# Making the low halves of weight chunks with an accumulating DMA instead of a VectorE subtraction

## The chip, the cores and the metric

One NeuronCore of a Trainium2 chip runs the whole program. The time is device microseconds from start to end of one execution; the number that counts is the median over several executions.

## What is computed

A two-layer encoder trunk on one sequence of 512 tokens, width 1024, all in float32. Each layer is a half-step SwiGLU feed-forward block (22 tiles of 128 hidden units), a token mixer (windowed attention beside dilated attention, 8 heads each) and a second feed-forward block. Every block is pre-normed and shifted, scaled and gated by vectors that come from a conditioning vector `c` (the "ada" weights):

```python
for l in range(DEPTH):
    mod = (c_act @ ada_w[l] + ada_b[l]).reshape(b, N_MOD, 1, D_MODEL)
    h = modulate(rmsnorm(x, norm_ffn1[l]), sh1, sc1)
    x = x + 0.5 * g1 * swiglu(h, ffn1_wi[l], ffn1_wo[l])
    h = modulate(rmsnorm(x, norm_mix[l]), sh2, sc2)
    x = x + g2 * token_mixing(h, cos, sin, w_in[l], sink[l], onorm_a[l], onorm_b[l], w_out[l])
    h = modulate(rmsnorm(x, norm_ffn2[l]), sh3, sc3)
    x = x + 0.5 * g3 * swiglu(h, ffn2_wi[l], ffn2_wo[l])
return rmsnorm(x, final_norm)
```

## The kernel before, in words

TensorE multiplies in a reduced float32 format, so every operand is split into a high part (the value rounded to that format) and a low part (the value minus its high part), and each product is three matmuls: high by high, low by high, high by low (`mm3`, lines 213 to 217). TensorE needs both parts of a weight.

**Weights come in chunks.** `specs` (lines 98 to 126) lists all weight chunks in the order of their use: 128 partitions by up to 1024 numbers, that is up to 512 KB. A *plain* chunk is one array; a *pair* is two, turned into more matrices by a recursive scheme (`emit_pair`, lines 153 to 195), which the change leaves alone. `emit_chunk` (lines 128 to 148) loads a plain chunk into a `raw` tile (4 buffers) through SP's DMA queue (line 142), makes `hi` on ScalarE (line 146) and `lo` on VectorE (line 147); `hi` and `lo` have 6 buffers each, shared with the pairs. The indexes in `finer` (line 105: three before and six after the start of each block) are done in two halves of 512.

**Which chunks there are.** Chunks 0 to 5 are converted by `start` (lines 903 to 938). Of the other plain ones 45 are in `finer` and 161 are not: 89 of 1024 columns, 64 of 896, 4 of 960 and 4 of 640. The first feed-forward block of layer 0 has no pairs at all: its chunks 6 to 64 are 59 of the 161. Every other feed-forward block has 21 to 24 of them (all `wo`), each mixer 18.

**What sets the order.** A scheduler lays down each engine's instruction order at build time, from the program order, priorities and buffer counts; at run time each engine's and each DMA queue's instructions issue in that order. SP issues all DMAs of the kernel before: weight chunks, the ada columns (`ada_col`, line 297, 4 `araw` buffers in the first block and one in the later ones), and in the mixers the copies that spread rotated queries and keys (lines 587 to 598). An ada column is multiplied by `c` and summed on VectorE (line 302); 73 of these loads fall into the first feed-forward block after its opening. GpSimd (POOL) does two elementwise operations per rotated query or key in the mixers (lines 577 and 581) and little else. `ahead` (line 206) emits the next chunks in program order, three ahead of use.

TensorE's results wait in 4 PSUM buffers `mm`; in feed-forward blocks ScalarE (`sg`, `gh`, lines 499, 507, 525) and VectorE (`x`, `sg`, `gl`, lines 366, 496, 506, 510) empty them.

Of the kernel before, what the change touches and what calls it, by code (L numbers as in the profile page):

```python
# [10 lines left out]
F32 = mybir.dt.float32  # L11
F32R = mybir.dt.float32r
I32 = mybir.dt.int32
AF = mybir.ActivationFunctionType
ALU = mybir.AluOpType
# [44 lines left out]
def tile_trunk(ctx: ExitStack, tc: tile.TileContext, xT, c, positions, adaT, cols, sink, wi1, wo1,  # L60
               wqk, wv, w_out, wi2, wo2, masks, freqs, out):
    nc = tc.nc
    V, A, T, G = nc.vector, nc.scalar, nc.tensor, nc.gpsimd
# [35 lines left out]
    finer = set()  # L99
    live = {}  # L100
# [27 lines left out]
    def emit_chunk(pieces=1):  # L128
        i = state["emit"]
        if i >= len(specs):  # L130
            return
        if isinstance(specs[i], tuple):
            for _ in emit_pair():
                pass
            return
        state["emit"] += 1
        ap = specs[i]
        n = ap.shape[1]
        raw = wp.tile([128, 1024], F32, tag="raw", name="raw", bufs=4)
        hi = wp.tile([128, 1024], F32R, tag="hi", name="hi")  # L140
        lo = wp.tile([128, 1024], F32R, tag="lo", name="lo")
        nc.sync.dma_start(raw[:, :n], ap)
        step = 512 if i in finer else n
        for a in range(0, n, step):
            sl = slice(a, min(a + step, n))
            A.activation(hi[:, sl], raw[:, sl], AF.Copy)  # L146
            V.tensor_tensor(lo[:, sl], raw[:, sl], hi.bitcast(F32)[:, sl], op=ALU.subtract)  # L147
        live[i] = (hi, lo)

    def parts(t):  # L150
        return [t[:, a:a + 512] for a in (0, 512)]
# [1 line left out]
    def emit_pair():  # L153


        i = state["emit"]
        state["emit"] += 1
        pool = temps[0]
        rg, ru = (wp.tile([128, 1024], F32, tag="raw", name="raw", bufs=4) for _ in range(2))
        for r, ap in zip((rg, ru), specs[i]):  # L160
            nc.sync.dma_start(r, ap)
        hs = [wp.tile([128, 1024], F32R, tag="hi", name="hi") for _ in range(3)]
        ls = [wp.tile([128, 1024], F32R, tag="lo", name="lo") for _ in range(3)]
        ta = pool.tile([128, 1024], F32, tag="ta", name="ta")
        h4 = pool.tile([128, 512], F32R, tag="h4", name="h4")
        l4 = pool.tile([128, 512], F32R, tag="l4", name="l4")
        live[i] = (*zip(hs, ls), (h4, l4))
        b11, b21 = parts(rg)
        b12, b22 = parts(ru)
        t1, t2 = parts(ta)  # L170

        def high(dst, src):
            for d, r in zip(parts(dst), parts(src)):
                A.activation(d, r, AF.Copy)  # L174

        def low(dst, src, h):
            V.tensor_tensor(dst, src, h.bitcast(F32), op=ALU.subtract)

        high(hs[0], rg)
        V.tensor_tensor(t1, b12, b11, op=ALU.subtract)  # L180
        yield
        V.tensor_tensor(t2, t1, b22, op=ALU.subtract)
        yield
        low(ls[0], rg, hs[0])
        yield
        high(hs[1], ta)
        V.tensor_tensor(b21, b21, t2, op=ALU.add)
        A.activation(h4, b21, AF.Copy)
        V.tensor_tensor(b12, b22, b12, op=ALU.subtract)
        low(ls[1], ta, hs[1])  # L190
        yield
        high(hs[2], ru)
        low(l4, b21, h4)
        yield
        low(ls[2], ru, hs[2])
# [3 lines left out]
    def chunk():  # L199
        i = state["use"]  # L200
        state["use"] += 1
        while state["emit"] <= min(i, len(specs) - 1):
            emit_chunk()
        return live.pop(i)

    def ahead(n=LA):
        while state["emit"] < len(specs):
            due = sum(3 if isinstance(specs[i], tuple) else 1 for i in range(state["use"], state["emit"]))
            if due > 1 if isinstance(specs[state["emit"]], tuple) else due >= n:
                return  # L210
            emit_chunk()
# [902 lines left out]
```

## Time and profile before

| what | value |
|---|---|
| median of 3 runs | 1957.17 us (1954.87 to 1959.26) |
| the profiled execution, its own time | 1955.42 us |
| its span, first to last instruction | 1953.6 us |
| mean granted TensorE clock | 0.993 of full speed |
| bytes moved by DMA | 267.98 MB, 41.8% of 16 engines' span on SP's queue |

The profiled execution is 1.8 us under the median, 0.09%. The span leaves 1.8 us of its own time outside the first and last instruction. Engine names in rows: PE is TensorE, PEld its weight loads, DVE VectorE, ACT ScalarE, POOL GpSimd, SPq the DMA queue that SyncE issues. A line number is that of the kernel. Matmul ends are modelled: a row's length holds the pipeline, while the distance of two starts tells the pace.

### The profile page before, as it was taken

How to read it: one execution, taken by the hardware profiler on the slowest of the kernel's cores; microseconds unless marked ns; L12 is line 12 of the kernel's file. 1: busy time of each engine (PE TensorE's matmuls, PEld its weight loads, DVE VectorE, ACT ScalarE, POOL GpSimd, SP SyncE). 2: the span in 40 equal slices, each digit the busy share in tenths (PEclk: the TensorE clock that was granted, in tenths of full speed). 3: DMA queues.
4: the chain of work that ended last, by engine and by line, in shares of the span. 5: the costliest groups of instructions: out<-in, count | busy, mean ns of one | idle time of the engine just before them, and what ended most of it. 6: DMA issues, size and time to landing. Idle time of an engine off the chain costs nothing.

```text
span 1953.6 us, 31187 instructions
## 1 busy us (share of the span) xinstructions
PE 1915.1 (98%) x12064; PEld 1718.1 (88%) x12064; DVE 1510.1 (77%) x2713; ACT 939.2 (48%) x1798; POOL 94.9 (5%) x69
## 2 busy tenths in 40 slices
PE   7999999999999999999999999999999999999998
PEld 5788888898778999989999897999977899898998
DVE  7988833477798988889589797876778989686773
ACT  5422222246585644536445262553556856353552
POOL 4000000011210000000000000000212000000000
PEclk8999999999999999999999999999999999999999
DMA  7889833244422154553415554242534113233231
GB/s 257 294 303 324 315 108 97 74 124 119 132 60 69 65 193 164 185 181 124 136 55 165 171 167 156 87 141 79 151 108 119 44 44 104 102 106 120 85 112 44
DMA packets 85111, 267.98 MB, mean 137 GB/s; under 512 B 10721, under 2 KB 13921, under 8 KB 84962
## 3 DMA queue, kind: packets, MB, share of 16 engines
q1 hardware_dynamic: 84962, 265.98, 41.8%
q8 instruction: 95, 1.56, 0.3%
q14 instruction: 54, 0.44, 0.1%
HBM read 244.97 MB, written 2.10 MB: 126 GB/s over the span
## 4 chain that ended last, share of the span: by engine, by line
PE 77%; DMA 9%; DVE 8%; issue 3%; ACT 2%; SPq 1%; POOL 0%; DVEq 0%; ACTq 0%; POOLq 0%
PE mm L217 14%; PE mm L216 14%; PE mm L215 14%; PE mm L457 9%; PE mm L458 8%; PE mm L459 8%; DMA araw<-in_adaT_dram 8%; DVE araw L302 3%; PE ptr L685 2%; DVE lo L147 1%; PE po L692 1%; PE po L693 1%; PE s L655 1%; PE s L656 1%; PE mm L624 1%
## 5 line engine op out<-in xcount | busy, mean ns | idle before, releaser
L146 ACT ACTIVATE hi<-raw 128x1024 fp32r<-128x1024 f32 (+5 forms) x251 | 213.8, 867 | 293.8 <-PE mm L217 201.8
L147 DVE TENSOR_TENSOR lo<-raw,hi 128x1024 fp32r<-128x1024 f32 (+5 forms) x251 | 258.1, 1039 | 74.3 <-ACT hi L146 73.4
L215 PE MATMUL mm<-hh,hi 128*128 128x512 f32 (+1 forms) x864 | 307.2, 357 | 7.4 <-ACT hh L286 6.8
L217 PE MATMUL mm<-hl,hi 128*128 128x512 f32 (+1 forms) x864 | 304.4, 357 | 2.7 <-DVE hl L287 2.7
L216 PE MATMUL mm<-hh,lo 128*128 128x512 f32 (+1 forms) x864 | 306.3, 356 | 0.0
L215 PE MATMUL mm<-gh,hi 128*128 128x512 f32 (+1 forms) x832 | 298.2, 358 | 5.5 <-ACT gh L507 5.5
L217 PE MATMUL mm<-gl,hi 128*128 128x512 f32 (+1 forms) x832 | 298.5, 359 | 0.5 <-DVE gl L441 0.2
L216 PE MATMUL mm<-gh,lo 128*128 128x512 f32 (+1 forms) x832 | 298.2, 358 | 0.0
L457 PE MATMUL mm<-sh,hi 128*128 128x256 f32 x912 | 260.4, 286 | 3.3 <-ACT sc L479 2.6
L458 PE MATMUL mm<-sh,lo 128*128 128x256 f32 x912 | 258.0, 283 | 0.0
L459 PE MATMUL mm<-sl,hi 128*128 128x256 f32 x912 | 257.9, 283 | 0.0
L302 DVE CUSTOM_DVE_ANT_0 araw<-araw,cs 128x1024 f32<-128x1024 f32 x136 | 167.7, 1236 | 57.9 <-DMA araw<-in_adaT_dram 57.5
L174 ACT ACTIVATE hi<-raw 128x512 fp32r<-128x512 f32 x228 | 132.9, 623 | 142.9 <-issue 74.3
L215 PEld LDWEIGHTS mm<-hh,hi 128*128 128x128 f32 x864 | 164.6, 191 | 29.9 <-ACT hh L286 8.1
L366 DVE SCALAR_TENSOR_TENSOR x<-mm,fin,x 128x512 f32<-128x512 f32 (+1 forms) x156 | 101.8, 653 | 114.3 <-PE mm L217 113.8
L217 PEld LDWEIGHTS mm<-hl,hi 128*128 128x128 f32 x864 | 164.1, 191 | 25.7 <-DVE hl L287 4.0
L215 PEld LDWEIGHTS mm<-gh,hi 128*128 128x128 f32 x832 | 157.8, 190 | 29.5 <-ACT gh L507 6.8
L216 PEld LDWEIGHTS mm<-hh,lo 128*128 128x128 f32 x864 | 164.5, 191 | 21.2
L217 PEld LDWEIGHTS mm<-gl,hi 128*128 128x128 f32 x832 | 158.1, 190 | 25.3 <-DVE gl L510 1.8
L457 PEld LDWEIGHTS mm<-sh,hi 128*128 128x128 f32 x912 | 174.1, 191 | 4.6 <-ACT sc L479 3.0
L216 PEld LDWEIGHTS mm<-gh,lo 128*128 128x128 f32 x832 | 158.1, 190 | 22.1
L458 PEld LDWEIGHTS mm<-sh,lo 128*128 128x128 f32 x912 | 174.3, 191 | 0.0
(188 smaller groups left out, 4043.7 us busy)
## 6 DMA issues: line engine op xcount, KB each, us to landing
raw<-in_wi_dram SPq DMA_DIRECT2D x170, 512.0 KB, 3.3
araw<-in_adaT_dram SPq DMA_DIRECT2D x144, 512.0 KB, 4.6
raw<-in_wo_dram SPq DMA_DIRECT2D x64, 448.0 KB, 4.1
raw<-in_wo_dram SPq DMA_DIRECT2D x32, 512.0 KB, 3.6
raw<-in_wqk_dram SPq DMA_DIRECT2D x26, 512.0 KB, 3.4
raw<-in_w_out_dram SPq DMA_DIRECT2D x16, 512.0 KB, 3.3
kh<-qh SPq DMA_DIRECT2D x40, 128.0 KB, 2.4
kl<-t SPq DMA_DIRECT2D x40, 128.0 KB, 2.3
```

The lines of the kernel that those rows point to most:

```text
L146: A.activation(hi[:, sl], raw[:, sl], AF.Copy)
L147: V.tensor_tensor(lo[:, sl], raw[:, sl], hi.bitcast(F32)[:, sl], op=ALU.subtract)
L174: A.activation(d, r, AF.Copy)
L215: T.matmul(ps, wh, X[0][:, s], start=start, stop=False)
L216: T.matmul(ps, wl, X[0][:, s], start=False, stop=False)
L217: T.matmul(ps, wh, X[1][:, s], start=False, stop=stop)
L302: return V.tensor_tensor_reduce(out=raw, in0=raw, in1=cs, scale=1.0, scalar=0.0, op0=ALU.mult, op1=ALU.add, accum_out=mod[:, l, ch, k:k + ...
L366: V.scalar_tensor_tensor(x[:, m, s], ps[:, s], gate[:, m:m + 1], x[:, m, s], op0=ALU.mult, op1=ALU.add)
L457: T.matmul(ps, wh, xh, start=start and k == 0, stop=False, skip_group_check=True)
L458: T.matmul(ps, wl, xh, start=False, stop=False, skip_group_check=True)
L459: T.matmul(ps, wh, xl, start=False, stop=stop and k == 3, skip_group_check=True)
L685: T.transpose(p[:, j * 128:j * 128 + 128], self.sm[qt][:, c0:c0 + 128], ident)
```

## The change

For plain chunks outside `finer`, `lo` is no longer a VectorE subtraction. ScalarE writes the high part of the raw chunk into `hi`, then the negated high part into `lo` (the same rounding with a scale of -1), and a DMA issued by GpSimd adds the raw chunk onto `lo`. The space for GpSimd's DMA descriptors is doubled. Chunks in `finer`, pairs and the first six chunks stay as they were.

```diff
@@ -140,12 +140,16 @@
         hi = wp.tile([128, 1024], F32R, tag="hi", name="hi")
         lo = wp.tile([128, 1024], F32R, tag="lo", name="lo")
         nc.sync.dma_start(raw[:, :n], ap)
-        step = 512 if i in finer else n
-        for a in range(0, n, step):
-            sl = slice(a, min(a + step, n))
+        live[i] = (hi, lo)
+        if i not in finer:
+            A.activation(hi[:, :n], raw[:, :n], AF.Copy)
+            A.activation(lo[:, :n], raw[:, :n], AF.Copy, scale=-1.0)
+            G.dma_start(lo.bitcast(F32)[:, :n], raw[:, :n], accum_op=ALU.add)
+            return
+        for a in range(0, n, 512):
+            sl = slice(a, min(a + 512, n))
             A.activation(hi[:, sl], raw[:, sl], AF.Copy)
             V.tensor_tensor(lo[:, sl], raw[:, sl], hi.bitcast(F32)[:, sl], op=ALU.subtract)
-        live[i] = (hi, lo)
@@ -1099,7 +1103,7 @@
-    nc = _bacc.Bacc("TRN2", target_bir_lowering=False, num_devices=1, dynamic_dma_scratch_size=1024)
+    nc = _bacc.Bacc("TRN2", target_bir_lowering=False, num_devices=1, dynamic_dma_scratch_size=2048)
```

## Rows read from the trace of the kernel before

**Rows 1.** The page, busy us of each engine (share of the span) xinstructions.

```profile
PE 1915.1 (98%) x12064; PEld 1718.1 (88%) x12064; DVE 1510.1 (77%) x2713; ACT 939.2 (48%) x1798; POOL 94.9 (5%) x69
```

**Rows 2.** Who waited for whom, TensorE: us in total, times, longest.

```profile
PE mm L215 <- ACT gh L507: 5.5, 3, 2.9
...
PE mm L457 <- ACT sc L479: 2.6, 2, 2.2
```

**Rows 3.** Stretches of 50 us: engines' busy us, then granted clock, DMA share, GB/s.

```profile
0.00:50.00 50.00, 34.63 (x129) 25.82 (x129) 39.69 (x65) 24.64 (x53) 21.60 (x16) 0.86 0.76 256
...
250.00:300.00 50.00, 50.00 (x222) 41.39 (x222) 18.57 (x20) 13.63 (x16) 0.00 (x0) 1.00 0.30 103
...
800.00:850.00 50.00, 47.71 (x302) 42.96 (x301) 40.27 (x62) 20.83 (x34) 0.00 (x0) 0.97 0.61 199
```

**Rows 4.** Groups by shape, lines 146 and 147: busy us, mean ns.

```profile
L146 ACT ACTIVATE hi<-raw 128x1024 fp32r<-128x1024 f32 x89 | 93.9, 1057 | 126.8 <-PE mm L217 93.7 <-issue 11.2 <-DMA raw<-in_wi_dram 7.5
L146 ACT ACTIVATE hi<-raw 128x896 fp32r<-128x896 f32 x64 | 60.8, 949 | 85.2 <-PE mm L217 59.9 <-PE mm L459 16.7 <-DMA raw<-in_wo_dram 5.3
L147 DVE TENSOR_TENSOR lo<-raw,hi 128x1024 fp32r<-128x1024 f32 x89 | 119.2, 1342 | 60.0 <-ACT hi L146 59.5
L147 DVE TENSOR_TENSOR lo<-raw,hi 128x896 fp32r<-128x896 f32 x64 | 69.5, 1086 | 11.6 <-ACT hi L146 11.4
```

**Rows 5.** DMA from 52 to 237 us: rate in 40 slices, share, issues.

```profile
GB/s 301 297 348 78 202 269 362 328 420 397 294 313 292 402 260 224 359 343 263 262 370 335 302 306 296 371 314 375 302 340 253 314 354 319 332 256 387 333 308 361
...
q1 hardware_dynamic: 16536, 57.88, 86.8%
...
araw<-in_adaT_dram SPq DMA_DIRECT2D x73, 512.0 KB, 6.1
raw<-in_wi_dram SPq DMA_DIRECT2D x25, 512.0 KB, 5.0
raw<-in_wo_dram SPq DMA_DIRECT2D x16, 448.0 KB, 4.6
```

**Rows 6.** DMA from 237 to 395 us: packets, MB, share of 16 engines.

```profile
q1 hardware_dynamic: 4361, 15.60, 30.8%
```

**Rows 7.** In order of time: the 41st chunk load after 52 us; its first matmul.

```profile
236.62 0.33 SPq L142 DMA_DIRECT2D raw<-in_wi_dram  x1
...
275.67 0.39 PE L215 MATMUL mm<-hh,hi 128*128 128x512 f32 x1
```

**Rows 8.** In order of time: chunks 6 to 8 converted; chunk 6 first used.

```profile
64.81 2.96 ACT L146 ACTIVATE hi<-raw 128x1024 fp32r<-128x1024 f32 x3 [1.89 <-PE mm L217]
...
65.97 3.50 DVE L147 TENSOR_TENSOR lo<-raw,hi 128x1024 fp32r<-128x1024 f32 x3 [2.26 <-ACT hi L146]
...
68.31 0.50 PE L215 MATMUL mm<-hh,hi 128*128 128x512 f32 x1 [0.58 <-ACT sg L525]
```

**Rows 9.** The page, DMA issues, copies inside SBUF: KB, us from issue to landing.

```profile
kh<-qh SPq DMA_DIRECT2D x40, 128.0 KB, 2.4
```

**Rows 10.** Stretches around a TensorE stall, columns as in rows 3.

```profile
828.00:832.00 4.00, 1.71 (x9) 1.09 (x8) 4.00 (x6) 1.26 (x2) 0.00 (x0) 1.00 0.83 252
832.00:834.00 2.00, 2.00 (x6) 1.25 (x5) 1.11 (x4) 0.43 (x1) 0.00 (x0) 0.59 0.96 317
834.00:836.00 2.00, 2.00 (x6) 1.57 (x6) 1.60 (x3) 0.52 (x1) 0.00 (x0) 0.56 0.60 231
```

**Rows 11.** In order of time: what VectorE did before that stall ended.

```profile
825.84 1.23 DVE L302 CUSTOM_DVE_ANT_0 araw<-araw,cs 128x1024 f32<-128x1024 f32 x1 [3.15 <-DMA araw<-in_adaT_dram]
...
827.33 1.08 DVE L147 TENSOR_TENSOR lo<-raw,hi 128x896 fp32r<-128x896 f32 x1
...
829.26 1.08 DVE L147 TENSOR_TENSOR lo<-raw,hi 128x896 fp32r<-128x896 f32 x1
...
831.66 0.50 PE L215 MATMUL mm<-gh,hi 128*128 128x512 f32 x1 [2.29 <-ACT gh L507]
```

**Rows 12.** Waits of SP's queue, 395 to 600 us (the first mixer).

```profile
SPq L142 <- DVE lo L147: 44.1, 11, 14.4
```

## The prediction

> **What bounds the kernel now.** I read the page's busy times first: TensorE is busy 98% of the span, 1915.1 of 1953.6 us, and VectorE only 77% [rows 1]. So all idle time of TensorE together is 38.5 us, and whatever VectorE is spared can give back at most that. Next the stretches: 15.4 us of it lie in the first 50 us, before any chunk that the change touches, and elsewhere TensorE is at 50 of 50 us except in a few places such as 800 to 850 [rows 3]. Then TensorE's waits: the long ones outside the opening are three for `gh` (5.5 us) and two for `sc` (2.6 us); none names `lo` [rows 2]. Last the DMA view: from 52 to 237 us, in the feed-forward block that has only plain chunks, the 16 DMA engines are 86.8% busy with 114 loads, 73 of them ada columns [rows 5], while from 237 to 395 us they are 30.8% busy [rows 6]. So: TensorE bounds everywhere, VectorE's subtraction is covered, and the one resource with little room, for 185 us, is the one that the change loads.
>
> **What is removed.** 161 subtractions on VectorE, 89 of them 119.2 us and 64 of them 69.5 us [rows 4], 189 us without the eight odd ones. Almost all of it is off the path. Where it is on it: at 827 and 829 two subtractions stand between a late ada column and the `gh` that TensorE waits 2.29 us for [rows 11], and behind such a stall the clock is granted at 0.59 and 0.56 for 4 us (half speed, 1.2 GHz, for most of it), which costs 0.41 + 0.44 of 2 us each, 1.7 us [rows 10]. Without the two subtractions (2.2 us) that stall is nearly gone: up to 4 us here, and as much at the other long `gh` wait (2.9 us, rows 2). But an accumulation on the engines makes that ada column land later by up to its own length (2.6 us, below) and VectorE stands in order behind it. I take half of it: -4 us for both; ends -8 and +8.
>
> **What is added on ScalarE.** 161 more conversions, by the rows of `hi` 93.9 + 60.8 us [rows 4], 155 us on an engine that is busy 939 of 1954 us [rows 1]. In a steady feed-forward stage it has 36 of 50 us free [rows 3]. I take 0; if that cover failed, one conversion of 1.06 us ahead of a `gh` or `sg` would show on TensorE, at most some 5 us over five blocks.
>
> **What is added on POOL and on SP's queue.** POOL is busy 5% [rows 1]; the 161 DMA issues wait there for ScalarE's negated copy, and in the mixers the two rotation operations of a query or key queue behind them. `raw` is freed when the accumulation has landed, not when VectorE is done, so SP's next chunk load waits longer, and the rotated copies stand behind it. In the first mixer SP already waits 11 times, 44.1 us, for that release [rows 12], without a TensorE wait to show for it. I take +1 us for each mixer; ends 0 and +5.
>
> **What is added on the DMA engines** is the large term. From 52 to 237 us, 86.8% of 185 us, 160.6 us, moved 57.88 MB [rows 5]: a 512 KB load (0.524 MB) takes 1.46 us of all 16 engines at that mean rate. In the four fullest slices of the same row (420, 397, 402 and 387 GB/s, mean 401.5) it takes 1.31 us. No row shows an accumulation. Lower bound: one pass, 1.31 us, since every byte crosses once. Nothing less: each issue moves its full tile. An accumulation, though, must read the raw tile and the old `lo` and write one tile, where a load reads one and writes one; I take two passes at the full rate, 2.62 us. Upper bound: three passes at the mean rate, 4.37 us. The Trainium skill ("Collectives: The Full Stack", The bandwidth ceiling: the fold count and why AG ≠ RS ≠ AR) says that a reduction in the DMA path is paced by its two source reads and runs at about half the rate of a copy. No run here shows it; by it the sum would be the one that I take. The Trainium skill also ("DMA: Bandwidth & Descriptors", Anatomy of one DMA — SWDGE (gpsimd) path) prices a GpSimd-issued DMA at about 2 us plus its bytes at 436 GB/s, an estimate of 1.2 us of engine time for 512 KB; no run here shows this for an accumulation, and by it the sum would be that of the hidden rival below.
>
> Now the stage. The 41 chunk loads up to 237 us (25 of 512 KB and 16 of 448 KB, that is 39 full ones) all become accumulations. The last of them is issued at 236.62 and TensorE first uses it at 275.67 [rows 7]: a lead of 39.0 us. From it go the load's landing, 5.0 [rows 5], two conversions, 2.1 [rows 4], and the accumulation's landing. A 128 KB copy inside SBUF lands after 2.4 us [rows 9], of which its bytes are 0.3 us at 401.5 GB/s, so 2.1 are fixed and the accumulation lands after 2.1 + 2.6 = 4.7. That leaves 27.2 us. At the full rate the loads need 57.88 / 0.4015 = 144.2 of the 185 us, leaving 40.8. Together 68 us of engine time can be had before TensorE must wait; the accumulations ask for 39 x 2.62 = 102. **TensorE then waits 34 us in this block.** This holds if SP keeps its order, with 73 ada columns ahead of that chunk. Ends: at one pass they need 51 us and nothing is lost; at two passes and the mean rate 114 against 52, +62 us; at three passes 170 against 52, +119 us (a little more lead is lost there, which I leave out). If the scheduler puts fewer ada columns ahead, the whole block counts: from 52 to 395 us, 343 us, 73.5 MB of loads need 183, so 160 are free (some 9 less for the last chunk), and 57 full accumulations need 149: loss 0. I take 34, from the order that the trace has.
>
> One wait is inside these 34 us and stands alone if the engines have room: the first handover. `hi` of chunk 6 can start only at 64.81, when a buffer comes free [rows 8]. Its negated copy is then done at 66.9, and the accumulation lands at 71.6; TensorE's second matmul of the chunk, its first with `lo`, would be due at 68.6. That is 3 us; 1.7 with a one-pass landing of 3.4 us.
>
> **Sum**: 34 + 2 - 4 + 0 = +32 us on the profiled execution's 1955.4 gives 1987 us. That execution is 1.8 us under the median shown, which is within the spread of the runs, so I don't correct for it. The difference that a measurement of this kernel can tell from none is about 0.2%, 3.9 us.
>
> **Rivals.** *Hidden* (same): the accumulation takes one pass, or the order of SP's queue spreads the ada columns over the block. Then 1.7 to 3 at the handover, 2 in the mixers and -4 from VectorE: 1955 to 1956 us. For it: DMA is 30.8% busy from 237 to 395 us, and the 39 us of lead. Against it: the 86.8%. It is also the case in which the change does not do for the time what it does for VectorE, because TensorE never waited for `lo`. *VectorE's relief counts* (faster): the stalls of 2.3, 2.9 and 2.2 us and the slow clock behind the first two go, 7.4 + 3.4 = 10.8 us, less the handover's 1.7: 1946 us. It decides if an accumulation costs less than 1.7 us, (40.8 + 27.2) / 39, and if ada columns land no later than now. For it: two subtractions lie in that very chain [rows 11]; against it: the same chain waits for an ada DMA first. *Slow accumulation* (slower still): three passes or more, +119 at the end, 2074 us; here 2040 and more. *Only the handover and the mixers* (slower): the engines have room, but handover, slow clock behind it, SP and POOL add 3 + 1.7 + 5, and VectorE's relief gives nothing: 1965 us.
>
> **How the numbers follow.** The forecast, the filled DMA engines at +5 to +80 us, gets 0.44; slow accumulation 0.10; handover and mixers alone 0.08; hidden 0.20; VectorE's relief 0.18. Slower is 0.44 + 0.10 + 0.08 = 0.62, same 0.20, faster 0.18. The predicted time is the forecast's, 1987; its own range is 1960 to 2035. For 8 in 10 the range goes down to 1948, which takes in the hidden case and about a third of the faster one (0.12 left out), and up to 2040, beyond which lies most of slow accumulation (0.08 left out).
>
> **What would show it.** In the changed profile, right: DMA share near 1.0 from about 65 us until the ada columns are done, well past 237 us; TensorE waits on `lo`'s DMA in chunks 6 to 50, each followed by a lower clock; an accumulation that takes about twice a load's engine time; no new waits from 400 us on beyond a few us. Wrong: TensorE at 50 of 50 us from 100 to 400 with DMA below 0.9, or accumulations landing in under 4 us under load; then the time is 1946 to 1956. Also wrong: TensorE losing its time in the mixers, on rotated copies behind POOL's or SP's waits, instead of in the first block.

## The result, and the profile after

The changed kernel takes 2104.55 us (median of 4 runs, 2096.9 to 2108.32) against 1956.12 of the kernel before, measured beside it (4 runs, 1954.87 to 1959.26): a ratio of 1.0751, 95% interval 1.0715 to 1.0787. I had said 1987 and a range up to 2040: the direction is right, but the loss is 148.4 us where I had 32.

The profiled execution takes 2096.9 us, its span is 2095.1. The page's busy times and DMA queues, to be read beside [rows 1]:

```profile
PE 1958.5 (93%) x12064; PEld 1746.7 (83%) x12064; DVE 1335.4 (64%) x2552; ACT 1078.4 (51%) x1959; POOL 230.7 (11%) x230
...
q1 hardware_dynamic: 84962, 265.98, 38.0%
q0 software_dynamic: 23184, 79.31, 20.1%
```

VectorE lost 175 us of work and its 161 subtractions, ScalarE gained 139 us net, and 79 MB more cross the DMA engines. TensorE's idle time rose from 38.5 to 136.6 us, and its busy time by 43 us for the same 12064 matmuls: behind a stall they run at the lower of the clock's two levels (1.2 GHz), so that the granted clock is 0.967 over the span and 0.76 in the worst stretch below. So the 141.5 us that the span grew are 98 us of TensorE waiting and 43 us of its matmuls running longer.

Where it waits is seen when the span is cut at the borders of the six blocks. A border is the first transposition `pR` of the block's normaliser, in order of time on TensorE; in the changed kernel:

```profile
455.54 0.38 PE L276 MATMUL pR<-ident,ny 128*128 128x128 f32 x2
715.53 0.41 PE L276 MATMUL pR<-ident,ny 128*128 128x128 f32 x2
1088.55 0.38 PE L276 MATMUL pR<-ident,ny 128*128 128x128 f32 x2
1466.69 0.38 PE L276 MATMUL pR<-ident,ny 128*128 128x128 f32 x2
1725.40 0.40 PE L276 MATMUL pR<-ident,ny 128*128 128x128 f32 x2
```

The same cut for every kernel of this study (us; FF1 is the feed-forward block with plain chunks alone, FF2 to FF4 are the later ones, M1 and M2 the mixers). Blocks that an edit does not touch repeat within some 2 us from run to run, FF2 within 4 and FF3 within 6:

| kernel | FF1 | M1 | FF2 | FF3 | M2 | FF4 | span |
|---|---|---|---|---|---|---|---|
| before | 392.6 | 244.1 | 352.6 | 358.1 | 243.8 | 362.4 | 1953.6 |
| after | 455.5 | 260.0 | 373.0 | 378.1 | 258.7 | 369.7 | 2095.1 |
| after - before | +62.9 | +15.9 | +20.4 | +20.0 | +14.9 | +7.3 | +141.5 |
| e1_first | 455.8 | 243.7 | 350.1 | 355.7 | 243.7 | 362.4 | 2011.5 |
| e2_mix | 392.7 | 261.4 | 351.8 | 355.6 | 259.3 | 362.3 | 1983.1 |
| e3_later_ffn | 394.1 | 243.7 | 377.7 | 375.8 | 244.5 | 367.4 | 2003.3 |
| e4_copy | 425.4 | 252.2 | 361.4 | 361.3 | 252.6 | 363.4 | 2016.3 |
| e5_short_ada | 415.9 | 261.5 | 364.3 | 366.8 | 260.5 | 368.1 | 2037.1 |
| e6_short_ada_before | 393.7 | 243.9 | 346.8 | 349.4 | 243.6 | 362.2 | 1939.6 |
| e7_raw8 | 454.0 | 243.7 | 353.1 | 354.8 | 244.0 | 362.3 | 2012.0 |
| e8_neg_only | 399.2 | 245.6 | 352.0 | 353.4 | 244.6 | 364.7 | 1959.5 |
| e9_no_ada_load | 455.2 | 262.3 | 358.3 | 354.3 | 256.8 | 370.8 | 2057.6 |
| e10_short_raw8 | 418.8 | 243.6 | 347.1 | 349.5 | 243.7 | 362.3 | 1965.0 |
| e11_mix_t2 | 392.3 | 257.6 | 351.6 | 354.4 | 256.1 | 362.3 | 1974.3 |
| e12_prefetch_before | 392.4 | 243.9 | 352.5 | 355.2 | 243.8 | 362.4 | 1950.2 |
| e14_late_first | 392.6 | 243.7 | 350.3 | 357.4 | 243.7 | 362.9 | 1950.6 |
| e15_mix_wout | 392.4 | 249.5 | 354.1 | 354.7 | 249.3 | 362.5 | 1962.5 |
| e16_pool_sub | 415.6 | 258.1 | 365.8 | 359.9 | 256.7 | 365.2 | 2021.2 |
| e17_no_add | 396.0 | 243.2 | 350.8 | 352.8 | 243.2 | 362.8 | 1948.7 |
| e18_mix_actq | 394.1 | 272.5 | 351.7 | 354.2 | 270.1 | 362.3 | 2004.9 |
| e19_actq_before | 393.4 | 260.5 | 351.6 | 352.4 | 261.7 | 362.1 | 1981.7 |

FF1, where I had put the whole loss, has 63 of the 141.5 us. The groups by shape answer to [rows 4] (line 145 is the high part, 146 the negated one):

```profile
L146 ACT ACTIVATE lo<-raw 128x1024 fp32r<-128x1024 f32 x89 | 94.0, 1057 | 131.8 <-PE mm L220 94.8 <-DMA raw<-in_wi_dram 18.4 <-PE mm L462 8.2
L145 ACT ACTIVATE hi<-raw 128x1024 fp32r<-128x1024 f32 x89 | 92.9, 1047 | 6.3 <-DMA raw<-in_wi_dram 6.3
...
L147 POOL DMA_DIRECT2D lo<-raw x161 | 140.4, 873 | 1610.7 <-ACT lo L146 1072.5 <-ACT sc L494 313.9 <-DVE part L579 132.4
```

These are as forecast: 161 more conversions of the known length. The stretches of FF1, as in [rows 3], show TensorE short of 50 us in four of six, and the DMA share at 1.0 until 300 us:

```profile
50.00:100.00 50.00, 42.00 (x166) 33.53 (x167) 34.22 (x67) 25.10 (x38) 8.99 (x9) 0.90 0.96 288
100.00:150.00 50.00, 38.50 (x158) 31.24 (x157) 21.30 (x35) 20.03 (x25) 7.79 (x9) 0.86 1.03 314
150.00:200.00 50.00, 50.00 (x222) 41.39 (x221) 20.77 (x37) 16.55 (x17) 6.93 (x8) 1.00 1.03 316
200.00:250.00 50.00, 41.40 (x162) 33.16 (x161) 26.97 (x48) 19.19 (x24) 6.92 (x8) 0.90 1.01 322
250.00:300.00 50.00, 29.49 (x108) 22.82 (x107) 27.23 (x47) 12.26 (x17) 4.31 (x5) 0.76 1.00 319
300.00:350.00 50.00, 50.00 (x222) 41.38 (x222) 6.49 (x12) 21.04 (x24) 8.68 (x10) 1.00 0.89 198
```

The DMA view of the stretch in which this block's ada columns are loaded, now 52 to 289 us where it was 52 to 237 [rows 5] (queue: packets, MB, share of 16 engines; then issues: KB, us to landing):

```profile
q1 hardware_dynamic: 16032, 56.05, 62.6%
q0 software_dynamic: 5184, 17.96, 38.7%
...
araw<-in_adaT_dram SPq DMA_DIRECT2D x72, 512.0 KB, 8.9
raw<-in_wi_dram SPq DMA_DIRECT2D x24, 512.0 KB, 7.9
lo<-raw POOLq DMA_DIRECT2D x22, 512.0 KB, 9.0
```

The 112 loads are nearly those that stood there before, at 62.6% of 237 us, 148 us. The 36 accumulations are new, 38.7%, 92 us for 17.96 MB, or 34.25 full ones: **2.68 us of all 16 engines each**. Together 240 us; the engines have nothing left, and the last ada column is issued 52 us later (289.27 instead of 237.00).

That is not how TensorE sees it. Its waits from 52 to 455 us, as in [rows 2], and then VectorE's, ScalarE's and SP's in the same stretch:

```profile
PE mm L219 <- ACT gh L444: 26.1, 2, 14.6
PE mm L219 <- DVE sg L530: 12.9, 3, 4.8
PE mm L220 <- DMA lo<-raw: 4.5, 2, 3.1
...
DVE araw L306 <- DMA araw<-in_adaT_dram: 102.5, 44, 5.9
...
ACT gh L444 <- DVE sg L530: 74.9, 10, 15.1
...
SPq L142 <- DMA lo<-raw: 226.2, 50, 10.8
```

The same waits in the kernel before, 52 to 392 us:

```profile
DVE araw L302 <- DMA araw<-in_adaT_dram: 16.8, 16, 2.5
...
ACT gh L440 <- DVE sg L526: 14.7, 9, 2.7
...
SPq L142 <- DVE lo L147: 203.0, 53, 5.6
```

TensorE waits 4.5 us for the low part and 39 us for `sg` and `gh`. ScalarE makes `gh` from VectorE's `sg` and waits 74.9 us for it, so both waits lead to VectorE; and VectorE has waited 102.5 us for ada columns. SP's wait for raw buffers is nearly as long before, where it costs TensorE nothing. One stall for `sg` in order of time:

```profile
226.41 1.23 DVE L306 CUSTOM_DVE_ANT_0 araw<-araw,cs 128x1024 f32<-128x1024 f32 x1 [3.40 <-DMA araw<-in_adaT_dram]
231.60 1.23 DVE L306 CUSTOM_DVE_ANT_0 araw<-araw,cs 128x1024 f32<-128x1024 f32 x1 [3.96 <-DMA araw<-in_adaT_dram]
...
234.10 0.68 DVE L530 TENSOR_TENSOR sg<-sg,mm 128x512 f32<-128x512 f32 x1
...
234.84 0.50 PE L219 MATMUL mm<-hh,hi 128*128 128x512 f32 x1 [4.75 <-DVE sg L530]
```

The product `sg` is 0.68 us of work that empties a PSUM buffer. It stands in VectorE's order behind five ada columns, each of which comes when the full engines bring it. Nothing that TensorE multiplies here was late itself. Of the last 56 columns of the block, one is issued 2.0 us after its buffer is free, on average (1.5 in the kernel before), and lands 9.1 us after its issue (6.1 before): the landing grew, not the wait in SP's queue.

### The profile page after: what moved, and what is told of

The parts are those of the page before. It is cut to its first block, busy times and chain, and to the rows that moved or that the text cites. A ratio compares the mean times of both kernels' runs of the same rounds, so it can differ in the third digit from the quotient of the medians.

```text
span 2095.1 us, 31655 instructions
## 1 busy us (share of the span) xinstructions
PE 1958.5 (93%) x12064; PEld 1746.7 (83%) x12064; DVE 1335.4 (64%) x2552; ACT 1078.4 (51%) x1959; POOL 230.7 (11%) x230
## 4 chain that ended last, share of the span: by engine, by line
PE 51%; DMA 20%; issue 13%; DVE 10%; ACT 3%; SPq 1%; POOL 1%; DVEq 0%; POOLq 0%; ACTq 0%
PE mm L221 11%; PE mm L219 11%; PE mm L220 11%; DMA araw<-in_adaT_dram 7%; DMA lo<-raw 6%; PE mm L461 4%; PE mm L462 4%; PE mm L463 4%; DMA raw<-in_wo_dram 4%; DMA qs<-t 2%; DVE lo L181 2%; DVE araw L306 2%; PE ptr L689 1%; PE po L696 1%; PE s L659 1%
## 5 line engine op out<-in xcount | busy, mean ns | idle before, releaser
L219 PE MATMUL mm<-gh,hi 128*128 128x512 f32 (+1 forms) x832 | 304.5, 366 | 36.7 <-ACT gh L444 26.1
L219 PE MATMUL mm<-hh,hi 128*128 128x512 f32 (+1 forms) x864 | 312.1, 363 | 22.5 <-DVE sg L530 12.9
L147 POOL DMA_DIRECT2D lo<-raw x161 | 140.4, 873 | 1610.7 <-ACT lo L146 1072.5
L220 PE MATMUL mm<-hh,lo 128*128 128x512 f32 (+1 forms) x864 | 310.7, 361 | 4.5 <-DMA lo<-raw 4.5
L221 PE MATMUL mm<-gl,hi 128*128 128x512 f32 (+1 forms) x832 | 303.0, 365 | 12.1 <-DVE gl L514 10.6
L220 PE MATMUL mm<-gh,lo 128*128 128x512 f32 (+1 forms) x832 | 302.7, 364 | 0.0
L461 PE MATMUL mm<-sh,hi 128*128 128x256 f32 x912 | 264.7, 290 | 18.8 <-ACT sc L483 9.8
L146 ACT ACTIVATE lo<-raw 128x1024 fp32r<-128x1024 f32 (+2 forms) x161 | 161.7, 1004 | 226.6 <-PE mm L220 143.1
L463 PEld LDWEIGHTS mm<-sl,hi 128*128 128x128 f32 x912 | 177.4, 195 | 0.0
```

The lines of the kernel that those rows point to most:

```text
L146: A.activation(lo[:, :n], raw[:, :n], AF.Copy, scale=-1.0)
L147: G.dma_start(lo.bitcast(F32)[:, :n], raw[:, :n], accum_op=ALU.add)
L219: T.matmul(ps, wh, X[0][:, s], start=start, stop=False)
L220: T.matmul(ps, wl, X[0][:, s], start=False, stop=False)
L221: T.matmul(ps, wh, X[1][:, s], start=False, stop=stop)
L461: T.matmul(ps, wh, xh, start=start and k == 0, stop=False, skip_group_check=True)
```

## The experiments

**The change in one place at a time.** Each kernel accumulates in some blocks and subtracts on VectorE, as before, in the others (`i` is the chunk's number, `starts[b]` the first of block `b`, and block(i) stands for `sum(s <= i for s in starts) - 1`). Each experiment is one run, except e12 and e17 with ten and e16 with four:

```diff
-        if i not in finer:
+        if i not in finer and i < starts[1]:                    # e1_first
+        if i not in finer and block(i) in (1, 4):               # e2_mix
+        if i not in finer and block(i) in (2, 3, 5):            # e3_later_ffn
```

> Accumulation only for chunks 6 to 64, the first feed-forward block; everything later subtracts on VectorE as before. Theory A, the 16 DMA engines are full in this block and each block pays for itself: the first block is 63 us longer as in the changed kernel, the others as before, 2018 us. Theory B, the loss of the later blocks is a loss carried over from this one (chunks that arrive late all the way): nearly all of the 148 us shows here, 2080 us or more.

> Accumulation only in the two mixers, 18 chunks each. Theory A, each block pays for itself, in the mixers by raw buffers freed later with SP's copies of queries and keys waiting behind the next chunk load: 15 us for each mixer, 1986 us, with VectorE waiting for those copies. Theory B, the mixers suffer only because they start with no chunks in hand after the first block: under 6 us in all, 1956 to 1962 us.

> Accumulation only in the three later feed-forward blocks (66 chunks of the last projection). Theory A, there accumulations delay ada columns for which VectorE waits in order: 20 us in each of the two blocks that load ada columns and at most 7 in the last one, which loads none, 2003 us. Theory B, the cost is that of every handover from pairs to these chunks, ada or not: the same 10 to 16 us in all three blocks, 1990 to 2003 us, with the last block no shorter than the others by over 5 us.

Against 1950.52 us of the kernel before on the same chip they took 2013.27 (+62.7), 1984.91 (+34.4) and 2005.08 (+54.6). The table shows that each loses in its own blocks what the whole change loses there, and nothing in the others. The three add up to 151.7 us, about the whole, 148.4 us between the medians. This is theory A in all three; FF2 lost 25 us in e3 where the theory had 20. So there are three places to explain, and no coupling between them beyond that spread; my forecast had put a loss worth naming only into the first.

**Half the bytes read.** The same DMAs as plain copies of the raw chunk over the low part (so the low part is the raw chunk):

```diff
-            G.dma_start(lo.bitcast(F32)[:, :n], raw[:, :n], accum_op=ALU.add)
+            G.dma_start(lo.bitcast(F32)[:, :n], raw[:, :n])
```

> All 161 chunks as in the changed kernel, but the DMA copies the raw chunk over the negated high part instead of adding it: same instructions, same waits, and each byte read once instead of twice (the low part is then the raw value, so the product is another). Theory A, engine time is what is short in the first block: a transfer takes about 1.4 us of all 16 engines instead of 2.74, 39 of them 55 us against 68 us to be had, so the first block loses 0 to 10 us instead of 63; the whole is under 2035 us. Theory B, landing times, buffers held longer and queues in order cost the time: a copy lands only some 1.3 us sooner than the 6.4 us of an accumulation, so at least two thirds of the first block's 63 us stay; the whole is 2060 us or more.

It took 2018.10 us, +67.6: in FF1 +32.8 instead of +62.9, in the mixers +8 and +9 instead of +16 and +15. The whole is under theory A's 2035, but FF1 lies between the two theories: over A's 10 and under B's 42. The DMA queues from 52 to 262 us, the stretch to this kernel's last ada column:

```profile
q1 hardware_dynamic: 16375, 57.31, 74.3%
q0 software_dynamic: 4288, 17.96, 20.8%
```

The same 17.96 MB take 20.8% of 210 us, 43.7 us or 1.28 us for a full copy, against 2.68 for an accumulation. The last ada column is issued at 259.83, 23 us later than before, where the accumulation made it 52; the block loses 33 and 63. In both, FF1 loses the delay of the ada columns and some 10 us more. That alone does not say which drives which: a late VectorE also frees the ada buffers late. VectorE's waits for ada columns in FF1 of e17 (below: the changed kernel without the DMA) and of e4 are, beside 102.5 in the changed kernel:

```profile
DVE araw L305 <- DMA araw<-in_adaT_dram: 30.4, 22, 3.0
```

```profile
DVE araw L306 <- DMA araw<-in_adaT_dram: 70.0, 45, 5.1
```

In these three kernels VectorE has the same number of reductions between two `sg`, and FF1 loses 3.4, 32.8 and 62.9 us. So some 27 to 40 us of waiting for ada columns are covered by VectorE's own idle time, and what goes beyond is lost nearly in full. (e7 below, with more buffers and a somewhat other order, loses 61.4 us at 120.3 of such waits, so this is no exact measure.)

**Fewer ada bytes.** Only 64 of 1024 elements of a column are loaded; VectorE's reduction keeps its length. In the changed kernel, and in the one before as its base:

```diff
-        nc.sync.dma_start(raw, adaT[l, ch * KD + k])
+        nc.sync.dma_start(raw[:, :64], adaT[l, ch * KD + k][:, :64])
...
-        return V.tensor_tensor_reduce(out=raw, in0=raw, in1=cs, scale=1.0, scalar=0.0, op0=ALU.mult,
+        return V.tensor_tensor_reduce(out=raw, in0=cs, in1=cs, scale=1.0, scalar=0.0, op0=ALU.mult,
```

> The changed kernel, but of every ada column behind the first sixteen only 64 of 1024 elements are loaded, and VectorE's reduction of the same length reads the silu row twice (so the modulation values are other ones); VectorE's work and the order stay. To be set against the kernel before with the same edit, block by block. Theory C (the accumulations fill the engines, the ada columns land late, VectorE stands in order behind them, and sg and gl with it): with 16 times fewer ada bytes the first feed-forward block loses at most 12 us (the handover among it) instead of 63, the second and third feed-forward blocks at most 8 instead of 20 each, the mixers still 15 each: the whole 45 to 55 over the kernel before with the same edit. Theory D (the loss is that raw buffers come free late and SP's queue stands in order, whatever the bytes): first block at least 35, second and third at least 12 each, the whole at least 95.

> The kernel before with the same short ada columns, the base for the run above. Theories C and D alike: TensorE lost 38.5 us in all before, about 15 of it in the opening, which this edit leaves; so 1942 to 1956 us.

2038.9 against 1941.35 us: the change now costs 97.6 us. FF1 loses 22.2 us instead of 62.9, so 41 us of it hung on the ada columns' bytes. That is most of it, but not down to theory C's 12, and under theory D's 35. FF2 and FF3 still lose 17.5 and 17.4, and the whole is over 95, both as theory D had it: in those blocks the ada columns' bytes are not it. The base alone came out 14.5 us faster than the kernel before, a little below what I had allowed.

In FF2 of e5 the 32 KB column is late all the same (order of time, SP's queue, then VectorE, then TensorE):

```profile
751.68 1.06 SPq L302 DMA_DIRECT2D araw<-in_adaT_dram  x1
...
758.53 1.22 DVE L303 CUSTOM_DVE_ANT_0 araw<-cs 128x1024 f32<-128x1024 f32 x1 [8.20 <-DMA araw<-in_adaT_dram]
...
766.69 0.68 PE L219 MATMUL mm<-gh,hi 128*128 128x512 f32 x1 [3.24 <-ACT gh L515]
```

This is where eight `wo` chunks are fetched in a burst with their accumulations. The column is issued at 751.68 and VectorE, after 8.20 us of waiting, starts on it at 758.53; `up`, `sg` and `gh` follow behind it.

**No ada loads in the later blocks.** The reductions stay, the loads go:

```diff
+        if n == 1:
+            return V.tensor_tensor_reduce(out=raw, in0=cs, in1=cs, scale=1.0, scalar=0.0, op0=ALU.mult,
+                                          op1=ALU.add, accum_out=mod[:, l, ch, k:k + 1]).ins
         nc.sync.dma_start(raw, adaT[l, ch * KD + k])
```

> The changed kernel, but in the feed-forward blocks behind the first mixer the 56 ada columns are not loaded at all; VectorE's reduction keeps its place and length and reads the silu row twice (the modulation values of the second layer are other ones). Theory C2 (what the later feed-forward blocks lose beyond the 6 us of the one block without ada columns is VectorE standing in order behind a column that lands late among accumulations, even a 32 KB one): the second and third feed-forward block, 17.5 us longer each than the kernel before with short columns (346.8 and 349.4 us), come to at most 9 us longer, 356 and 358 or less. Rival F (the eight wo chunks in a burst, their accumulations and the buffers they hold, cost this with or without ada columns): at least 14 us longer, 361 and 363 or more. First block and mixers as in the changed kernel, 455 and 259 us.

FF2 and FF3 came to 358.3 and 354.3 us, 11.5 and 4.9 longer than e6. FF3 is where C2 put it, FF2 between the two theories. Together the loss fell from 34.9 to 16.4 us (over e6, which still loads the short columns): about half of what FF2 and FF3 lose is VectorE behind a late column. The rest stays without any ada load, and FF4, which has none, loses 5 to 8 us in all these kernels. In FF2 of e9 VectorE waits 14.5 us for raw chunks of the pairs, where it waits 1.3 in the kernel before; that this is the rest was not tested.

**More raw buffers.** SP waits 226 us for raw buffers in FF1. Eight instead of four:

```diff
+        if 6 <= i < starts[1] - 3 and i % 8 >= 4:
+            raw = temps[0].tile([128, 1024], F32, tag="rawx", name="raw", bufs=4)
+        else:
+            raw = wp.tile([128, 1024], F32, tag="raw", name="raw", bufs=4)
```

> The accumulation in the first feed-forward block alone (+63 us there), with eight raw buffers instead of four for its plain chunks. Theory C: the same bytes cross the same full engines and the ada columns stay late; the block loses 50 to 68 us. Theory D: SP no longer waits for raw buffers, and the loss falls to at most 30.

> The first block alone with the accumulation, with short ada columns (64 of 1024 elements loaded, other modulation values) and eight raw buffers for its plain chunks; to be set against the kernel before with short columns, whose first block takes 393.7 us. With short columns and four buffers the block was 22 us longer; with full columns, eight buffers did nothing (454.0 against 455.8). Theory G (two covers, one behind the other: first the engines' bytes, and once those are gone SP's queue, in which the ada columns stand behind chunk loads that wait for a raw buffer): at most 9 us longer, the handover and little else. Rival H (the accumulations' own 2.86 us of all engines each keep even the 32 KB columns late, whatever SP's order): at least 17 us longer.

With full columns, FF1 took 454.0 against e1's 455.8. But the edit did not take SP's wait away (e7, 52 to 454 us; 228.4 in e1):

```profile
SPq L147 <- DMA lo<-raw: 167.1, 35, 25.7
```

So 61 us less of it gave back 1.8 us. That, the 203.0 us of the same wait in the kernel before, and the time from free buffer to issue above speak against theory D in FF1; this run alone does not exclude it. With short columns FF1 took 418.8, 25.1 longer than e6 and no better than e5's 22.2 (SP still waits 180.1 us, 195.0 in e5, so theory G was hardly tried). That is past theory H's bound, but its cause is not shown by it either. VectorE's work in the 15 us ahead of the longest stall of e10 (11.31 us for `gh`), and in the 11 us of one step of e6 (line, form, count | busy, mean ns):

```profile
L309 DVE CUSTOM_DVE_ANT_0 araw<-cs 128x1024 f32<-128x1024 f32 x10 | 11.9, 1219 | 2.4 <-DMA araw<-in_adaT_dram 2.4
```

```profile
L299 DVE CUSTOM_DVE_ANT_0 araw<-cs 128x1024 f32<-128x1024 f32 x6 | 7.3, 1224 | 0.0
```

Nine of the ten reductions stand in VectorE's order between two `sg` (at 124.36 and 138.58), 11 of 14 us, and it waits only 2.4 us for columns. The changed kernel has four or five at this place, and so has e17, whose FF1 loses 3.4 us. So the residue of e5 and e10 is at least in part this other order, which comes from the edit and is no part of the changed kernel's 63 us. These two runs bound the part of the ada bytes (at least 41 us of 63) and do not settle the rest.

**Only where the engines have room.** The accumulation for chunks 44 to 64 of FF1 alone:

```diff
-        if i not in finer:
+        if i not in finer and 44 <= i < starts[1]:
```

> The accumulation only for the first block's chunks 44 to 64, 21 of its 59, which are loaded from about 237 us on, after the last ada column; all other chunks as before. Theory C (it costs only where ada columns want the same engines at the same time): the block takes 392 to 395 us, the whole 1950 to 1959. Rival K (each accumulation costs by itself, 63 us / 59 = 1.07 us): 22 us more, the block 412 to 417.

1952.96 us, FF1 392.6: nothing lost. Its DMA queues from 237 to 400 us, [rows 6] with 21 accumulations in it:

```profile
q0 software_dynamic: 3024, 11.01, 37.1%
q1 hardware_dynamic: 4588, 16.40, 33.1%
...
lo<-raw POOLq DMA_DIRECT2D x21, 512.0 KB, 5.9
```

A third of the block's accumulations, 2.88 us of all engines each (37.1% of 163 us, by 21), landing after 5.9 us, cost nothing where the engines are 33% busy with loads and no ada column waits. Rival K falls for this block. Which of the two conditions counts, this run does not separate.

**The mixers.** In e2 the first long stall is this (order of time):

```profile
422.35 0.60 SPq L597 DMA_DIRECT2D qs<-t  x1
...
428.93 0.69 DVE L583 TENSOR_TENSOR t<-mm,rc 128x512 f32<-128x512 f32 x1 [9.31 <-DMA qs<-t]
429.77 0.44 PE L631 MATMUL mm<-hi,hh 128*128 128x320 f32 x1 [4.74 <-DVE t L583]
```

The copy out of `t` is issued at 422.35 and over at 428.93, 6.6 us, where [rows 9] have 2.4; two accumulations were issued at 422.00, just ahead of it. VectorE wants to overwrite `t`, and TensorE stands behind it. This copy is one of the latest: over the first mixer of e2 the median landing of the rotated copies is 3.4 to 3.8 us, where it is 2.3 to 2.4 before. So a second buffer for `t`:

```diff
-            t1 = pool.tile([128, S], F32, tag="t1", name="t1")
+            t1 = pool.tile([128, S], F32, tag="t1", name="t1", bufs=2)
```

> The accumulation in the two mixers alone (261.4 and 259.3 us there, against 243.9), with two buffers instead of one for t, the rotated row that the next rotation overwrites. Theory I (the rotated copies are issued on time but land after 6.5 us instead of 2.4 among accumulations, and VectorE, then TensorE, wait for t): with the second buffer VectorE need not wait, and a mixer loses at most 9 us. Rival J (the copies themselves, kh and kl before the scores, and the late lo, hold TensorE just as long): at least 13 us.

The mixers took 257.6 and 256.1 us: 3 to 4 us less than in e2, still 13.5 and 12.3 over the kernel before. By these times rival J is right in the first, and all but right in the second. But the second buffer did not clear the wait: in the first mixer VectorE's wait for the copies out of `t` fell from 13.2 to 6.1 us, and TensorE still waits 5.1 us for `t` (4.7 in e2), and longer for other copies (`kl<-t`, 4.5 us instead of 2.9). So theory I's size was not tried cleanly. Then only the last matrix of the mixer:

```diff
+        if i not in finer and block(i) in (1, 4) and i - starts[block(i)] >= 19:
```

> The accumulation only for the mixers' last weight matrix, 5 of a mixer's 18 accumulations; the query, key and value chunks as before. Theory I (the loss belongs to the projections, where the rotated copies land among accumulations): a mixer takes at most 245.5 us against 243.9. Rival K (each accumulation costs alike, 16 us / 18): 4.4 us more, 248 or so.

249.5 and 249.3 us, 5.5 for five accumulations: rival K's 4.4 is the nearer. In the mixers the loss is spread, about 1 us for each accumulation, and is not the projections' alone. Last, the copies on another queue, so that none stands behind a chunk load:

```diff
-                nc.sync.dma_start(sf[lo, 0], qh[lo])
+                nc.scalar.dma_start(sf[lo, 0], qh[lo])
```

> The accumulation in the two mixers alone, with the rotated copies of queries and keys issued on ScalarE's queue instead of SP's; to be set against the run without accumulation and with the same edit. Theory M (SP's order: a copy stands behind a chunk load that waits for a raw buffer until an accumulation has landed): the difference falls from 15 or 17 us to at most 7 a mixer. Rival N (the copies are issued in time and land late among accumulations, so that their order does not matter): at least 12 us.

> The kernel before with the rotated copies issued on ScalarE's queue, the base for the run above: mixers of 242 to 250 us, the rest as before.

The base missed its expectation: without any accumulation the edit costs 17 us a mixer (260.5 and 261.7). Over it the accumulation adds 12.0 and 8.4, the first at rival N's bound, the second between. SP's order is at most part of it, as far as a base that loses so much itself can tell. In the mixers the accumulations are shown to be the cause (e2, e17), and half the engine time costs half as much (e4); by which waits they cost it stays open.

**VectorE's relief and ScalarE's load.** Three kernels without the DMA: the subtraction kept behind both conversions (e8), nothing in its place (e17), GpSimd's subtraction in its place (e16):

```diff
-            G.dma_start(lo.bitcast(F32)[:, :n], raw[:, :n], accum_op=ALU.add)
+            V.tensor_tensor(lo[:, :n], raw[:, :n], hi.bitcast(F32)[:, :n], op=ALU.subtract)   # e8_neg_only
```

```diff
-            A.activation(lo[:, :n], raw[:, :n], AF.Copy, scale=-1.0)
-            G.dma_start(lo.bitcast(F32)[:, :n], raw[:, :n], accum_op=ALU.add)
+            G.tensor_tensor(lo[:, :n], raw[:, :n], hi.bitcast(F32)[:, :n], op=ALU.subtract)   # e16_pool_sub
```

> ScalarE's added work alone: both conversions as in the changed kernel, then VectorE's subtraction over it in place of the accumulation. My prediction's term for this was 0, at most 5 us. Theory C and D alike: 1953 to 1960 us, no block over 2 us longer. If ScalarE's added 162 us count by themselves (rival E: gh is late because ScalarE is): 10 us or more, in the feed-forward blocks.

> The changed kernel without the accumulating DMA: the low part stays minus the high part, the raw chunk is not added. VectorE is relieved, ScalarE has both conversions, no byte more crosses the DMA engines. ScalarE's part alone took 5.4 us in one run. If VectorE's relief gives 4 us as my term had it: 1952 to 1959 us. If it gives 10.8: 1944 to 1951. Under theory C nearly the whole of the change's +147 us must be gone, so 1965 us at most; if ScalarE's in-order negated copies had a large part in the loss, 1980 or more.

> A candidate that relieves VectorE without a DMA: GpSimd subtracts hi from raw for the same 161 chunks (a 128x512 operation there took 1.3 us, so about 2.6 us for a chunk, some 400 us in all on an engine that is busy 95). If VectorE's relief counts as my rival had it (10.8 us): 1942 to 1948 us. If it counts as my term had it (4 us): 1948 to 1954. If the rotation's two GpSimd operations and the low parts, which come 1.3 us later, hold TensorE in the mixers: 1958 us and more.

e8 took 1961.27 us, 5.4 over the kernel before beside it, mostly in FF1 (+6.6). That misses the forecast for this run (1960 at most, no block over 2 us), is just past the end that I had given ScalarE's term, and is half of the least that rival E asked for. e17 gives a ratio of 1.0005 (0.9989 to 1.0021). Its page:

```profile
PE 1914.5 (98%) x12064; PEld 1716.7 (88%) x12064; DVE 1333.0 (68%) x2552; ACT 1077.6 (55%) x1959; POOL 90.8 (5%) x69
```

VectorE has 177 us less to do than in [rows 1] and TensorE is as busy as before: ScalarE's load and VectorE's relief together are worth nothing that can be measured. And since this kernel differs from the changed one by the accumulating DMA alone, that DMA is the whole loss: its bytes, its issue on GpSimd and the buffers that it holds, taken together. e16, the candidate, takes 1.0351 times as long (1.0332 to 1.0370): the third case, though not in the mixers alone (FF1 +23, the mixers +14 and +13, FF2 +13). The last section shows a cause for FF1.

**A better kernel?** In e6 short columns gave back 14.5 us, so I tried to load the later ada columns one step ahead in the kernel before:

```diff
+            if pend:
+                raw, l, ch, k = pend.pop()
+                ada_red(raw, l, ch, k)
...
+                nc.sync.dma_start(raw, adaT[l, ch * KD + k])
+                pend.append((raw, l, ch, k))
```

> A candidate: the kernel before, without accumulation, whose later ada columns are loaded one step ahead of their reduction, in the same single buffer. In the kernel before, short columns gave back 5.8 and 8.7 us in the second and third feed-forward block and nothing elsewhere. If that is VectorE's wait for the landing: 1942 to 1951 us. If the load one step earlier is late all the same: 1952 to 1959 us.

A ratio of 0.9991 (0.9978 to 1.0003): the second of the two cases. No kernel of this study with the whole computation is measurably faster than the one before.

## Why the prediction was wrong, point by point

**What bounds the kernel** was right: TensorE, with VectorE's subtraction covered, and the DMA engines of FF1 as the resource with little room.

**The accumulation's price** was right: two passes, 2.62 us at the full rate, measured 2.68 in the full stretch and 2.88 in e14. The Trainium skill's rule that I set beside it ("Collectives: The Full Stack", The bandwidth ceiling: the fold count and why AG ≠ RS ≠ AR), half the rate of a copy for two source reads, is stated there of collectives; e4 agrees with it: 1.28 us against 2.68. The landing was right only where there is room: I had 4.7 us, it is 4.7 in the first mixer of e2, 5.9 in e14 and 9.0 in the full stretch. The Trainium skill's price for a GpSimd-issued DMA ("DMA: Bandwidth & Descriptors", Anatomy of one DMA — SWDGE (gpsimd) path), an estimate of 3.2 us here, is below all three.

**FF1, +34 forecast, +62.9 measured.** The failed step is the wait, and with it "That leaves 27.2 us", the lead that I added to the room of the engines: I had TensorE wait for a chunk's `lo`, with that chunk's 39 us of lead as cover. It waits 4.5 us for `lo` and 39 us for `sg` and `gh`, which stand in VectorE's order behind ada columns. An ada column has no such lead, only its four buffers: VectorE waits for some of them even before (16.8 us). What covers a late column is VectorE's idle time, and beyond that the delay is lost. Without the lead my own sum reads 102 - 40.8 = 61 us, but that it meets 62.9 is in part luck: the same sum for e4, 39 x 1.28 - 40.8 = 9 us, is far from the 33 us lost there, with the engines 95% busy (74.3 + 20.8) and not full. My end of +62, two passes at the mean rate, met it by luck too: the price came out near the full rate's, and the lead is still in that sum. The handover, 3 us inside, is there: 3.1 is the longest of the waits for `lo`.

**The mixers, +2 forecast, +30.8 measured.** The failed step is "I take +1 us for each mixer; ends 0 and +5". I read [rows 12] as a queue with slack, because SP's waits there showed no TensorE wait. The copies of 128 KB, which share the engines with 2.8 us accumulations, were priced as before, at 2.4 us. The runs showed medians of 3.4 to 3.8 us, 6.6 for one in e2's stall, and a loss of about 1 us for each accumulation; which waits make it up is open.

**The ada-delayed chains, -4 forecast, +47.7 measured in FF2 to FF4.** I had seen the mechanism (an accumulation "makes that ada column land later by up to its own length (2.6 us, below) and VectorE stands in order behind it"), and halved it against a gain from the missing subtractions: the failed step is "I take half of it: -4 us for both; ends -8 and +8". The runs show no such gain (e17), and the delay comes at the `wo` bursts with several accumulations at a time, not one; VectorE's wait for ada columns in FF2 is 38.4 us, 20.4 before. About half of FF2's and FF3's loss goes with the ada loads (e9); the cause of the other half is open.

**ScalarE at 0** holds to a few us (e8, e17). **POOL's issues** stand in no run without the DMA that they issue, so their part is not shown.

**The rivals.** VectorE's relief (1946) is excluded by e17. Hidden failed in FF1 and holds only where e14 put the work. Slow accumulation, 2040 and more, holds the time that came, but by another way than three passes. My range ended at 2040 because every part outside FF1 had ends of a few us, taken from a kernel in which these waits cost TensorE little.

**What I said would show it:** the DMA share near 1.0 well past 237 us and an accumulation of twice a load's time came true; waits on `lo` in chunks 6 to 50 did not; and "no new waits from 400 us on", which was to be right, is wrong by 78.5 us. Time lost in the mixers on rotated copies, which I had among the signs of being wrong, came too, but beside the loss of the first block and not instead of it.

## What to carry to other kernels

Taking work off an engine that TensorE does not wait for was worth nothing here, and what replaced it was paid on a shared resource. When a change adds DMA traffic, list every small transfer and every load that an in-order engine waits for with little lead: here they, more than the transfers that were added, turned busy DMA engines into lost time. A lead belongs to one stream; it may not be lent to another that stands in the same queue.

## What the runs showed of the hardware

An accumulating DMA inside SBUF takes 2.68 to 2.88 us of all 16 engines for 512 KB, a plain one of GpSimd 1.28; its landing is 4.7 us in the first mixer of e2, 5.9 in e14 (4.8 for the chunk loads from `wi` in the same stretch) and 9.0 in the full one.

GpSimd's subtraction slows VectorE. In e16, VectorE's ada reductions by form, and GpSimd's subtractions (count | busy us, mean ns):

```profile
L305 DVE CUSTOM_DVE_ANT_0 araw<-araw,cs 128x1024 f32<-128x1024 f32 x136 | 218.3, 1620 | 59.7 <-DMA araw<-in_adaT_dram 59.6
...
L146 POOL TENSOR_TENSOR lo<-raw,hi 128x1024 fp32r<-128x1024 f32 x89 | 222.5, 2502 | 474.5 <-ACT hi L145 473.9
```

The reduction took 1236 ns in the kernel before and 1620 here; the residual update, which reads PSUM, kept its 748 ns. The Trainium skill ("GPSIMD Engine Reference", Specifications) says that GpSimd's SBUF interfaces are shared with VectorE and contended by instructions with two SBUF inputs; these rows agree. FF1 lost 23 us without a byte more on the DMA engines; TensorE's long waits there are for `gh` (15.9 us) and none is for the low part, which fits a slower VectorE, though no run takes this apart further.

Issuing the rotated copies on ScalarE's queue instead of SP's cost 17 us a mixer with no accumulation anywhere (e19), though a copy's median landing stayed at 2.3 to 2.4 us.
